# Shifted rows of a convolution loaded place and channel first, shift last, and issued by SP: an encoder trunk on one core

## The chip, the cores and the metric

The kernel runs on one core of one Trainium2 chip. The metric is device time in microseconds (us) of one execution, by the median of several runs. One more execution was taken with the hardware profiler; all rows below are of that one.

The engines have the names of the profile: PE is TensorE's matrix multiplication and PEld its weight load, DVE is VectorE, ACT is ScalarE, POOL is GpSimd. SP, SyncE, computes nothing and issues DMAs. A name with q (SPq, POOLq) is that engine's queue of instructions. Each engine works through its own instructions in order; a DMA, once issued, runs on the core's 16 DMA engines.

## The reference

A trunk of two layers on x of 512 tokens by 1024 channels, float32. Each layer is a half-step SwiGLU FFN, a token mixer, a second half-step FFN; every part has an RMSNorm before it and a residual add. Layer 0 mixes by a Conformer convolution, layer 1 by a bidirectional HGRN2 recurrence. The change lies in the convolution alone:

```python
def conformer_conv(h, w_pw1, b_pw1, w_dw, b_dw, ln_g, ln_b, w_pw2, b_pw2):
    a, gate = jnp.split(h @ w_pw1 + b_pw1, 2, axis=-1)
    u = a * jax.nn.sigmoid(gate)
    u = lax.conv_general_dilated(          # depthwise: 31 taps along the tokens
        u, w_dw[:, None, :], window_strides=(1,), padding=[(15, 15)],
        dimension_numbers=("NWC", "WIO", "NWC"), feature_group_count=1024) + b_dw
    u = layer_norm(u, ln_g, ln_b)
    return jax.nn.silu(u) @ w_pw2 + b_pw2
```

## The kernel before, in words

Channels lie on the 128 partitions, in 8 blocks of 128 (KD); the 512 tokens lie along the free dimension. Every weight matrix is split into a high and a low part (`split`, L137: a cast on ACT at L138, a subtraction on DVE at L139), and each product is three matmuls (`mm3`, L195, with lines L196 to L198). Weight chunks of up to 1 MB come through three buffers, issued by SP at L133 (`wdma`), about two chunks ahead of use. The high and low parts have three buffers each, so that a cast waits for matmuls of three parts ago.

The parts run one after the other: `ffn(0)`, `conv`, `ffn(1)`, `ffn(2)`, `hgrn`, `ffn(3)`.

In `conv` (L679) a loop over the 8 blocks j makes two projections of 24 matmuls each (`proj`, L415), `pa` and the gate `pg`. Then `evac` (L706) makes the gated block `u` on DVE and ACT, with even and odd tokens apart (L711 to L714); that of j = 0 is held until the statistics of the RMSNorm are there, after the third projection. `u` is 128 channels by 2 phases by 272 places.

The depthwise convolution is done by PE: for that, one partition has to hold one pair of place group and channel group at one of four shifts. `evac` gets this by a way over DRAM. It stores `u` to a DRAM tile `ud` of 32 rows (L721; the profile writes `ud<-u`), a row being one of 2 phases and one of 16 channel groups (CG), with 8 channels of 272 places (row = 2176 values). It then loads `u8` from it (L724; the profile writes `u<-ud`, leaving out the digit): each of the 32 rows four times, from four starting places one value apart, 2173 values each, which makes 128 partitions. `u8` has three buffers, `ud` two. POOL issues both for j = 0 to 6, and SP for j = 7. POOL also builds `w8` (L726), the taps' weights spread to a block form.

`taps_of` (L733) then runs 64 matmuls on PE in the profile (L738, 128x256 each) and puts their result, plus bias, into `y` (L752 or L754); `y` is stored into the `v` tiles (L776). Sums of `y` and its square are kept on POOL (`s1`, `s2`, L768 and L769) and brought over the partitions by small matmuls (`sums`, L780, line L789).

The order is set by `hook` (L795): after the fourth k of the first projection of a turn j, the oldest `u8` that waits in `ready` is taken, if there are two, so the taps of block j run in turn j + 2. The last three run behind the loop, with the sums of `s1` and `s2` ahead of the last (L805 to L808). The framework that builds the program may move an instruction some places against this order on its engine. After the last sums come the layer norm (L817 to L834), and `k_outer` with the second pointwise weights.

On the host, `_layout` (L1225) arranges the tap weights `tw` and the selection `ch` to fit the order of partitions of `u8`.

Of the kernel before, what the change touches and what calls it, by code (L numbers as in the profile page):

```python
# [18 lines left out]
P = 128  # L19
D = 1024  # L20
S = 512
KD = D // P
# [25 lines left out]
SH, CG = 8, 16  # L48
NG, NW = P // CG, 4
NM = 272  # L50
# [15 lines left out]
def tile_encoder(ctx: ExitStack, tc: tile.TileContext, xT, vecs, masks, w13, w2, pw1, kout, kout2, win, win_i, taps, out):  # L66
    nc = tc.nc
# [40 lines left out]
    for w_ in win_order:  # L108
        n = int(w_[1:])
# [153 lines left out]
    def col(c):  # L263
        return vec[:, c:c + 1]
# [122 lines left out]
    def rs():  # L387
        return norm["rs"]
# [290 lines left out]
    def conv(next_prep):  # L679
# [3 lines left out]
        with tc.tile_pool(name="cv", bufs=1) as cv, ExitStack() as scratch:  # L683
# [15 lines left out]
            def ap(t, off, dims, part=True):  # L699
                a = t[:]  # L700
                return bass.AP(a.tensor, a.offset + off, ([list(a.ap[0])] if part else []) + dims)

            def pairs(t):
                return t.rearrange("p (b h) -> p b h", h=2)

            def evac(j, pa, pg):  # L706
                ta = tp.tile([P, S], F32, name="t0", tag="t0")
                tg = tp.tile([P, S], F32, name="t1", tag="t1")
                sg = tp.tile([P, S], F32, name="t2", tag="t2")
                u = us[j % 3]  # L710
                nc.vector.tensor_tensor(tg, pg, rs(), op=ALU.mult)  # L711
                nc.scalar.activation(sg, tg, AF.Sigmoid, bias=col(C_BPW1 + 8 + j))
                nc.vector.tensor_tensor(ta, pa, rs(), op=ALU.mult)
                nc.vector.scalar_tensor_tensor(ap(u, 7, [[1, T2], [NM + 1, 2]]), pairs(ta), col(C_BPW1 + j), pairs(sg),  # L714
                                               op0=ALU.add, op1=ALU.mult)


                row = NG * NM
                e = nc.sync if j == KD - 1 else nc.gpsimd
                ud = dr.tile([2 * CG, row], F32, name="ud", tag="ud")  # L720
                e.dma_start(ap(ud, 0, [[NM, P], [CG * row, 2], [1, NM]], False), u)  # L721
                u8 = cp.tile([P, row], F32, name="u8", tag="u8", bufs=3)
                n = row - SH // 2 + 1
                e.dma_start(u8[:, :n], ap(ud, 0, [[1, SH // 2], [row, 2 * CG], [1, n]], False))  # L724
                w8 = cp.tile([P, NG * NW, 2 * CG], F32, name="w8", tag="w8", bufs=2)
                nc.gpsimd.tensor_tensor(w8.rearrange("p n (c h) -> p n c h", h=2),  # L726
                                        ap(cw, T_CH, [[0, NG * NW], [2, CG], [1, 2]]),
                                        ap(cw, T_W + j * NG * NW * 2, [[2, NG * NW], [0, CG], [1, 2]]), op=ALU.mult)
                ready.append((j, u8, w8))
# [70 lines left out]
            for j in range(KD):  # L800
                pa = proj(lead, xh, xl, hook)
                pg = proj(lead, xh, xl, hook)
                lead.evac(lambda j=j, pa=pa, pg=pg: evac(j, pa, pg))
# [421 lines left out]
def _layout(x, norm_g, ffn_w13, ffn_w2, conv_w_pw1, conv_b_pw1, conv_w_dw, conv_b_dw, conv_ln_g, conv_ln_b,  # L1225
            conv_w_pw2, conv_b_pw2, hgrn_w_in, hgrn_lb, hgrn_gn_g, hgrn_w_out, final_g):


    def cols(a):
        a = np.asarray(a).reshape(-1, KD, P)  # L1230
        return a.transpose(2, 0, 1).reshape(P, -1)

    lb = np.asarray(hgrn_lb).transpose(1, 0, 2)


    n = np.arange(D)
    back = n // P * P + n % 32 // 2 * NG + n % P // 32 * 2 + n % 2
    p, k, g, w, h = np.ix_(np.arange(P), np.arange(KD), np.arange(NG), np.arange(NW), np.arange(2))
    wpad = np.pad(np.asarray(conv_w_dw)[0], ((1, 2), (0, 0)))
    tw = wpad[SH * w + p // 32 * 2 + 1 - p % 32 // CG - h + 1, k * P + p % CG * NG + g].reshape(P, -1)  # L1240
    p1, c1 = np.meshgrid(np.arange(P), np.arange(P), indexing="ij")
    same = p1 % 2 == c1 % 2
    ch = p1[:, :2 * CG] % CG == c1[:, :2 * CG] // 2
    p, k, h = np.ix_(np.arange(P), np.arange(KD), np.arange(2))
    tb = np.asarray(conv_b_dw)[0][k * P + p % 32 // 2 * NG + p // 32 * 2 + h].reshape(P, -1)
    taps = np.concatenate([tw, same, ch, tb, same[:, :2]], axis=1, dtype=tw.dtype)
    vecs = np.concatenate([cols(norm_g), cols(final_g), cols(conv_b_pw1), cols(np.asarray(conv_ln_g)[..., back]),
                           cols(np.asarray(conv_ln_b)[..., back]), cols(conv_b_pw2), cols(lb), cols(hgrn_gn_g)], axis=1)
    s, t = np.meshgrid(np.arange(P), np.arange(P), indexing="ij")
    masks = np.zeros((P, 7, P), np.float32)  # L1250
    for l in range(7):
        masks[:, l] = (s ^ t) >> l == 1
    w13 = np.asarray(ffn_w13).reshape(4, NP, 2, P, 2, NFF, P).transpose(0, 5, 3, 4, 2, 1, 6).reshape(4, NFF, P, 2 * D)
    w2 = np.asarray(ffn_w2).reshape(4, 2, HALF, P, KD, P).transpose(0, 1, 4, 3, 2, 5).reshape(4, 2, KD, P, HALF * P)
    pw1 = np.asarray(conv_w_pw1)[0].reshape(KD, P, 2, KD, P).transpose(3, 1, 2, 0, 4).reshape(KD, P, 2 * D)
    kw = np.stack([np.asarray(conv_w_pw2)[0][back], np.asarray(hgrn_w_out)[0]]).reshape(2, 4, 2, P, KD, P)
    kout = kw[:, :, :, :, :NOUT].transpose(0, 1, 3, 2, 4, 5).reshape(2, 4, P, 2 * NOUT * P)
    kout2 = kw.reshape(2, KD, P, KD, P)[:, :, :, NOUT:].transpose(0, 2, 3, 1, 4).reshape(2, P, 2 * D)
    wi = np.asarray(hgrn_w_in)[0].reshape(KD, P, 5, NH, P)
    win = wi[:, :, [0, 2, 3, 4]].reshape(KD, P, 2, 2, NH, P).transpose(4, 2, 1, 3, 0, 5).reshape(NH, 2, P, 2 * D)  # L1260
    win_i = np.asarray(hgrn_w_in)[0][:, D:2 * D].reshape(2, 4, P, 2, S).transpose(3, 0, 2, 1, 4)
    win_i = win_i.reshape(4, P, 2 * D)
    xT = np.asarray(x)[0].T.reshape(KD, P, S)
    arrays = dict(xT=xT, vecs=vecs, masks=masks.reshape(P, 7 * P), w13=w13, w2=w2, pw1=pw1, kout=kout, kout2=kout2,
                  win=win, win_i=win_i, taps=taps)
    return {k: np.ascontiguousarray(v) for k, v in arrays.items()}
# [19 lines left out]
```

## Time and profile before

| | |
|---|---|
| runs | 2082.84, 2089.87, 2090.8 us; median 2089.87 |
| the profiled execution | 2090.77 us, of which the span is 2089.0 |
| PE busy | 1965.5 us (94%) |
| DVE busy | 1457.9 us (70%) |
| ACT busy | 964.9 us (46%) |
| POOL busy | 156.0 us (7%) |
| mean granted TensorE clock | 0.972 of full speed |
| loads of `u8` on POOL | 7 of 1086.5 KB, median 23.4 us from issue to landing |

The span is the time from the first to the last instruction that the profiler shows. Busy shares are means over the whole span: stages with different limits lie in them. DMA-issuing instructions are not counted as busy. "Landing" is the end of a transfer, counted from its issue. The granted clock is the share of full TensorE clock that the throttle allowed in a stretch.

### The profile page before, as it was taken

How to read it: one execution, taken by the hardware profiler on the slowest of the kernel's cores; microseconds unless marked ns; L12 is line 12 of the kernel's file. 1: busy time of each engine (PE TensorE's matmuls, PEld its weight loads, DVE VectorE, ACT ScalarE, POOL GpSimd, SP SyncE). 2: the span in 40 equal slices, each digit the busy share in tenths (PEclk: the TensorE clock that was granted, in tenths of full speed). 3: DMA queues.
4: the chain of work that ended last, by engine and by line, in shares of the span. 5: the costliest groups of instructions: out<-in, count | busy, mean ns of one | idle time of the engine just before them, and what ended most of it. 6: DMA issues, size and time to landing. Idle time of an engine off the chain costs nothing.

```text
span 2089.0 us, 31116 instructions
## 1 busy us (share of the span) xinstructions
PE 1965.5 (94%) x12767; PEld 1758.1 (84%) x12767; DVE 1457.9 (70%) x2207; ACT 964.9 (46%) x1593; POOL 156.0 (7%) x129
## 2 busy tenths in 40 slices
PE   8999999667589999999999999999999999999997
PEld 7998998544367998998998999888888878989996
DVE  7965975323158965978994796568857878947964
ACT  5643653211045643654662464345545545634642
POOL 2000001122101000001000000111101110000002
PEclk9999999888789999999999999999999999999998
DMA  5223233333312223223223232321111121233221
GB/s 192 81 84 108 101 100 113 121 93 97 106 66 81 102 84 109 101 100 113 96 95 104 101 108 91 117 79 61 61 62 71 43 89 61 99 105 110 102 97 55
DMA packets 40274, 196.47 MB, mean 94 GB/s; under 512 B 6740, under 2 KB 13268, under 8 KB 24132
## 3 DMA queue, kind: packets, MB, share of 16 engines
q1 hardware_dynamic: 33092, 181.57, 25.3%
q0 software_dynamic: 4480, 10.56, 1.9%
q10 hardware_dynamic: 2560, 2.36, 0.4%
q8 instruction: 100, 1.64, 0.3%
q14 instruction: 42, 0.34, 0.0%
HBM read 188.04 MB, written 4.33 MB: 92 GB/s over the span
## 4 chain that ended last, share of the span: by engine, by line
PE 65%; DVE 5%; issue 1%; ACT 1%; DVEq 0%; ACTq 0%
PE mm L511 28%; PE mm L196 9%; PE mm L198 9%; PE mm L197 9%; PE aux L983 3%; PE mm L444 2%; DVE wlo L139 1%; PE mm L886 1%; PE mm L888 1%; PE mm L887 1%; PE aux L1055 1%; DVE x7l L460 1%; PE aux L292 0%; ACT whi L138 0%; DVE bl L460 0%
## 5 line engine op out<-in xcount | busy, mean ns | idle before, releaser
L511 PE MATMUL mm<-x7h,whi 128*128 128x256 f32 x1944 | 546.7, 282 | 7.1 <-ACT mm L524 3.5
L511 PE MATMUL mm<-x7h,wlo 128*128 128x256 f32 x1944 | 545.2, 281 | 2.4 <-DVE wlo L139 2.3
L511 PE MATMUL mm<-x7l,whi 128*128 128x256 f32 x1944 | 545.6, 281 | 1.4 <-DVE x7l L158 1.4
L138 ACT CAST whi<-wraw 128x1024 fp32r<-128x1024 f32 (+2 forms) x297 | 274.3, 924 | 362.2 <-PE mm L197 311.7
L139 DVE TENSOR_TENSOR wlo<-wraw,whi 128x1024 fp32r<-128x1024 f32 (+2 forms) x297 | 324.3, 1092 | 144.9 <-ACT whi L138 140.3
L511 PEld LDWEIGHTS mm<-x7h,whi 128*128 128x128 f32 x1944 | 366.2, 189 | 10.1 <-ACT mm L524 4.4
L511 PEld LDWEIGHTS mm<-x7h,wlo 128*128 128x128 f32 x1944 | 366.2, 189 | 3.6 <-DVE wlo L139 3.6
L511 PEld LDWEIGHTS mm<-x7l,whi 128*128 128x128 f32 x1944 | 366.4, 188 | 2.2 <-DVE x7l L158 2.0
L196 PE MATMUL mm<-gh,whi 128*128 128x512 f32 (+1 forms) x715 | 276.0, 386 | 0.0
L198 PE MATMUL mm<-gh,wlo 128*128 128x512 f32 (+1 forms) x715 | 275.9, 386 | 0.0
L197 PE MATMUL mm<-gl,whi 128*128 128x512 f32 (+1 forms) x715 | 275.9, 386 | 0.0
L138 ACT CAST whi<-s 128x1024 fp32r<-128x1024 f32 x162 | 169.9, 1049 | 168.3 <-PE mm L511 117.3
L139 DVE TENSOR_TENSOR wlo<-s,whi 128x1024 fp32r<-128x1024 f32 x162 | 197.9, 1222 | 40.7 <-ACT whi L138 40.1
L370 POOL TENSOR_TENSOR ss<-ss,sq 128x512 f32<-128x512 f32 x48 | 67.0, 1396 | 1465.7 <-ACT sq L369 1464.9
L198 PEld LDWEIGHTS mm<-gh,wlo 128*128 128x128 f32 x715 | 134.3, 188 | 27.1
L196 PE MATMUL mm<-xh,whi 128*128 128x512 f32 x384 | 156.8, 408 | 0.0
L196 PEld LDWEIGHTS mm<-gh,whi 128*128 128x128 f32 x715 | 134.3, 188 | 26.6
L197 PEld LDWEIGHTS mm<-gl,whi 128*128 128x128 f32 x715 | 134.3, 188 | 26.3
L198 PE MATMUL mm<-xh,wlo 128*128 128x512 f32 x384 | 152.3, 397 | 0.0
L197 PE MATMUL mm<-xl,whi 128*128 128x512 f32 x384 | 150.8, 393 | 0.0
L158 DVE TENSOR_TENSOR s<-wraw 128x512 f32<-128x512 f32 x162 | 110.5, 686 | 8.5 <-DMA wraw<-in_w 6.6
L638 DVE TENSOR_TENSOR t<-mm,rs 128x512 f32<-128x512 f32 x63 | 43.5, 691 | 104.4 <-PE mm L198 104.4
(245 smaller groups left out, 3223.0 us busy)
## 6 DMA issues: line engine op xcount, KB each, us to landing
wraw<-in_w SPq DMA_DIRECT2D x87, 1024.0 KB, 4.8
wraw<-in_w SPq DMA_DIRECT2D x64, 704.0 KB, 4.1
wraw<-in_win SPq DMA_DIRECT2D x16, 1024.0 KB, 4.8
wraw<-in_pw SPq DMA_DIRECT2D x8, 1024.0 KB, 4.8
u<-ud POOLq DMA_DIRECT2D x7, 1086.5 KB, 23.4
wraw<-in_kout SPq DMA_DIRECT2D x8, 768.0 KB, 7.1
wraw<-in_win_i SPq DMA_DIRECT2D x4, 1024.0 KB, 4.6
x<-in_xT SPq DMA_DIRECT2D x8, 256.0 KB, 6.0
```

What stands on the lines that cost most here:

```text
L138: nc.scalar.copy(hi[:, a:b], raw[:, off + a:off + b])
L139: nc.vector.tensor_tensor(lo[:, a:b], raw[:, off + a:off + b], hi[:, a:b].bitcast(F32), op=ALU.subtract)
L158: nc.vector.tensor_tensor(o, a, b, op=op)
L196: nc.tensor.matmul(o, lhsT=wh, rhs=ah, start=first, stop=False)
L197: nc.tensor.matmul(o, lhsT=wh, rhs=al, start=False, stop=False)
L198: nc.tensor.matmul(o, lhsT=wl, rhs=ah, start=False, stop=last)
L370: nc.gpsimd.tensor_tensor(norm["ss"], norm["ss"], sq, op=ALU.add)
L444: nc.tensor.matmul(o[:, x[0]], lhsT=wt[:, sl], rhs=x[at], start=k == 0 and wt is w[0] and at == 1 and x is ops[0], stop=k == KD - 1 and wt ...
L460: nc.vector.scalar_tensor_tensor(l, xs[k][:, c], col(gc + k), h.bitcast(F32), op0=ALU.mult, op1=ALU.subtract)
L511: nc.tensor.matmul(o, lhsT=a[:, sl], rhs=b[kp][:, x], start=start and kp == 0 and a is w[0] and b is x7h, stop=kp == NP - 1 and a is w[1], ...
L638: nc.vector.tensor_tensor(pn, p, norm["rs05"], op=ALU.mult)
L983: nc.tensor.matmul(sp[:, c * P:(c + 1) * P], lhsT=kp[:, c * P:(c + 1) * P], rhs=view(Q, hl, c), start=True, stop=True)
```

## The change

The load of `u8` reads the same values, in another order of partitions: before, the shift was the slowest index (partition = 32 x shift + row), after, the row is (partition = 4 x row + shift). The store and the load of every block are issued by SP. The host tables follow the new order of partitions; their sizes stay.

```diff
                 row = NG * NM
-                e = nc.sync if j == KD - 1 else nc.gpsimd
                 ud = dr.tile([2 * CG, row], F32, name="ud", tag="ud")
-                e.dma_start(ap(ud, 0, [[NM, P], [CG * row, 2], [1, NM]], False), u)
+                nc.sync.dma_start(ap(ud, 0, [[NM, P], [CG * row, 2], [1, NM]], False), u)
                 u8 = cp.tile([P, row], F32, name="u8", tag="u8", bufs=3)
                 n = row - SH // 2 + 1
-                e.dma_start(u8[:, :n], ap(ud, 0, [[1, SH // 2], [row, 2 * CG], [1, n]], False))
+                nc.sync.dma_start(u8[:, :n], ap(ud, 0, [[row, 2 * CG], [1, SH // 2], [1, n]], False))
...
-    tw = wpad[SH * w + p // 32 * 2 + 1 - p % 32 // CG - h + 1, k * P + p % CG * NG + g].reshape(P, -1)
+    tw = wpad[SH * w + p % 4 * 2 + 1 - p // 64 - h + 1, k * P + p // 4 % CG * NG + g].reshape(P, -1)
...
-    ch = p1[:, :2 * CG] % CG == c1[:, :2 * CG] // 2
+    ch = p1[:, :2 * CG] // 4 % CG == c1[:, :2 * CG] // 2
```

## Rows read from the trace of the kernel before

**Rows 1.** The page: granted TensorE clock in 40 equal slices, in tenths.

```profile
PEclk9999999888789999999999999999999999999998
```

**Rows 2.** Waits, 355 to 680 us: who waited for whom, us in total, times, longest.

```profile
PE mm L738 <- DMA u<-ud: 73.3, 7, 20.7
...
POOL u L724 <- DMA ud<-u: 63.7, 7, 20.6
```

**Rows 3.** Groups by line, 365 to 582 us: the taps matmuls.

```profile
L738 PE MATMUL mm<-u,w 128*32 128x256 f32 x512 | 44.8, 516 | 73.3 <-DMA u<-ud 73.3
```

**Rows 4.** PE in order of time: start us, us; in brackets idle time before.

```profile
394.23 0.39 PE L197 MATMUL mm<-xl,whi 128*128 128x512 f32 x1
394.45 0.39 PE L198 MATMUL mm<-xh,wlo 128*128 128x512 f32 x1
413.46 4.91 PE L738 MATMUL mm<-u,w 128*32 128x256 f32 x64 [18.62 <-DMA u<-ud]
...
449.83 0.39 PE L198 MATMUL mm<-xh,wlo 128*128 128x512 f32 x1
...
535.06 0.39 PE L198 MATMUL mm<-xh,wlo 128*128 128x512 f32 x1
536.84 3.66 PE L738 MATMUL mm<-u,w 128*32 128x256 f32 x64 [1.39 <-DMA u<-ud]
...
569.77 1.87 PE L789 MATMUL aux<-cw,s 128*128 128x2 f32 x8 [2.46 <-POOL s L768]
...
574.36 6.36 PE L738 MATMUL mm<-u,w 128*32 128x256 f32 x62
```

**Rows 5.** POOL in order of time, its stores and loads.

```profile
388.61 0.77 POOL L721 DMA_DIRECT2D ud<-u  x1 [12.27 <-DVE u L714]
...
392.91 0.76 POOL L721 DMA_DIRECT2D ud<-u  x1 [0.66 <-DVE u L714]
...
453.71 0.79 POOL L721 DMA_DIRECT2D ud<-u  x1 [6.35 <-DVE u L714]
```

**Rows 6.** SP's queue in order of time.

```profile
397.04 0.33 SPq L133 DMA_DIRECT2D wraw<-in_pw  x1
...
448.47 0.33 SPq L133 DMA_DIRECT2D wraw<-in_pw  x1
...
538.24 0.38 SPq L721 DMA_DIRECT2D ud<-u  x1
540.71 0.67 SPq L724 DMA_DIRECT2D u<-ud  x1
```

**Rows 7.** Landing of the DMAs of L721, L724, and L133 (365 to 585).

```profile
DMA to landing us min/median/max: 2.3/8.2/21.1
...
DMA to landing us min/median/max: 21.8/23.4/24.9
...
DMA to landing us min/median/max: 4.6/12.4/13.6
```

**Rows 8.** Windows: length, engines' busy us, granted clock, DMA share, GB/s.

```profile
272.00:274.00 2.00, 2.00 (x19) 2.00 (x18) 1.97 (x3) 0.57 (x1) 0.00 (x0) 1.00 0.91 385
...
365.00:585.00 220.00, 142.35 (x952) 102.43 (x950) 56.62 (x77) 34.22 (x43) 44.83 (x39) 0.81 0.37 101
...
404.00:410.00 6.00, 0.00 (x0) 0.00 (x0) 0.00 (x0) 0.00 (x0) 0.00 (x0) 0.50 0.27 102
546.00:560.00 14.00, 0.00 (x0) 0.00 (x0) 0.00 (x0) 0.00 (x0) 0.00 (x0) 0.50 0.51 121
```

**Rows 9.** DMA issues by line: size of each, median us to landing.

```profile
wraw<-in_pw SPq DMA_DIRECT2D x8, 1024.0 KB, 4.8
...
u<-ud POOLq DMA_DIRECT2D x7, 1086.5 KB, 23.4
...
ud<-u SPq DMA_DIRECT2D x1, 272.0 KB, 2.3
```

**Rows 10.** ACT in order of time: the cast of a weight part.

```profile
500.31 1.05 ACT L138 CAST whi<-wraw 128x1024 fp32r<-128x1024 f32 x1 [4.37 <-PE mm L197]
```

## The prediction

> **What bounds the kernel now.** I read the page first. The slices show the granted TensorE clock at 9 tenths nearly everywhere and a dip to 7 and 8 in slices 8 to 12 [rows 1]: something starves TensorE between about 365 and 600 us, and that is the convolution (L679), where every changed line runs. So the argument is made in that stage alone.
>
> Next the waits from 355 to 680 us. On PE one dominates: the taps matmuls of L738 wait for the DMA that fills `u8`, seven times, 73.3 us, the longest 20.7 [rows 2]. The groups by line from 365 to 582 us give the matmuls' own time: 512 in 44.8 us, that is 5.6 us for each of the eight `taps_of` [rows 3]. The order of PE's work shows what that should be: with 1.39 us of idle time before them, 64 took 3.66 us; after 18.62 us of idle time 4.91 [rows 4]. While PE sits idle the clock falls: in 404 to 410 and in 546 to 560, with no matmul at all, the granted clock is 0.50, the lower of the two levels (1.2 against 2.4 GHz) [rows 8]. So the late loads cost twice, as waits and as slow taps.
>
> Then, why the loads are late. On POOL the first store goes at 388.61, the second at 392.91 with the first load between them, a later one at 453.71 [rows 5]. A load took 21.8 to 24.9 us to land, a store 2.3 to 21.1, median 8.2, and the load always waits for its store [rows 7]. The windows say why the load is slow: from 404 to 410, with this one load in flight, the sixteen DMA engines were busy 0.27 of the time and moved 102 GB/s, which is four engines' worth; from 546 to 560, with two such loads in flight, 0.51 and 121 GB/s; yet from 272 to 274, in a weight load, 0.91 and 385 GB/s [rows 8]. The load's outermost dimension in L724 is the shift, of size 4. A weight chunk of nearly the same size (1024 against 1086.5 KB) lands in 4.8 us, the load in 23.4 [rows 9].
>
> The Trainium skill, DMA: Bandwidth & Descriptors, section "Why a DMA increments its semaphore by 16 and not by 1", says a DMA runs on the largest number of engines, up to 16, that divides the slowest dimension of both sides. By that the old order gets 4 and the new (32 outermost) gets 16; the trace agrees on the 4, and no run yet shows the 16.
>
> **The change part by part.**
>
> *The order of the load.* Same bytes, same 128 rows of 8.7 KB, but place and channel (32) outermost and shift innermost. Lower bound for the load: a weight chunk's 4.8 us [rows 9], 5.1 for 1086.5 KB. Upper bound: nothing gained, 23.4. Between: if what holds two loads at 121 GB/s is not the number of engines but the small region that they read, 1.11 MB take 9.2 us. Quartering 23.4 for four times the engines gives 5.9. I take 5.9, near the weight chunk, because per engine 102 GB/s over four is what 385 GB/s over sixteen is (25 and 24).
>
> *Issue on SP.* Seven stores and seven loads leave POOL for SP; the eighth pair is on SP already. On SP that store (272 KB) landed in 2.3 us [rows 9], with the load following 2.47 us after it (538.24, 540.71) [rows 6]; I take 2.5. POOL loses 7 x 2 issues and 63.7 us of waiting between them [rows 2], and nothing on POOL sets the end, so I cost that at nothing; what hides it is that POOL's sums for `s1`, `s2` are needed only at L807.
>
> On SP each load waits for its store, and behind the waiting load stand the weight loads of L133. Pair j can be issued about 3.7 us after the second projection of j (last matmul 449.83 to 450.06, store 453.71) [rows 4, 5], the weight chunk of that turn goes out earlier, at 448.47 [rows 6]; a chunk behind the pair would be held for at most 2.5 us plus two issues. That chunk's second half was first cast in the turn that ends at 500.31 [rows 10]: 52 us later, and still about 30 at the faster pace below. I cost it at nothing.
>
> *When the data is wanted.* From the end of the second projection of j to taps j, PE has 60 projection matmuls (12 up to taps j - 1, the other 36 of that turn, 12 of the next; the starts 394.23 and 394.45 are one step apart, 0.227 us over a run of them, so 13.6 us [rows 4]) and one taps block of 3.66: 17.3 us. The chain to be hidden is 3.7 (to the store) + 2.5 + 0.1 + load. With 5.9 it is 12.2, so there is no wait in the middle, with 5.1 us to spare; a load of up to 11.0 us would do. Now it is about 3.7 + 8.2 + 0.3 + 23.4 = 35.6, which is why each turn waits. VectorE is no bound in place of it: 56.6 us busy in the 220 from 365 to 585 [rows 8], against some 130 that the stage would still take.
>
> *First taps.* Store at 388.4, load at 390.9, landed at 396.8; PE stops at 394.84 as before [rows 4]: 2.0 us left of 18.62.
>
> *Last taps.* The second projection of j = 7 ends at 535.29. Chain to the last taps: 2.95 (store at 538.24) + 2.5 + 5.9 = 11.3 us. Before them PE has two taps blocks (7.3), then waits 2.46 us for POOL's sum as now and runs 16 small matmuls of L789 (1.87 for the first eight at the low clock, perhaps half that at the high one) [rows 4]: about 0.6 us of wait is left, and the L789 give back some 1.9.
>
> **The sum.** Waits 73.3, less 2.0 at the first taps: 71.3. Taps at full clock: 44.8 - 8 x 3.66 = 15.5. Around the last taps: 1.9 - 0.6 = +1.3. Together 88 us. The profiled execution took 2090.77 (span 2089.0, 1.8 around it), 0.9 above the median of the three runs shown (2089.87). 2090.8 - 88 = 2002.8. I forecast **2003 us**. What comes after (from 581 us) is moved, not changed.
>
> Own range: with the load at 5.1, 1.5 less; if the clock also stays high over the short gaps ahead of the pointwise projection, 2 x 1 us on L292 and some 3 on its first matmuls less: 1997. With 9.2, 3.3 us at each end and some slow matmuls: 2011. If on SP the first pair stands behind the weight chunk that went out at 397.04 [rows 6], 6 to 8 us more: 1997 to 2016.
>
> **The rivals.**
>
> *Same queue, same ring (12 in 100).* Pairs and weight chunks now share SP's queue. On POOL one store took 21.1 us to land, the longest; the second, at 392.91, was issued right behind the first load and is the one that fits [rows 5, 7]: it stood behind that load. If each pair stands behind a whole weight chunk (4.8), the chain is 17.0 against 17.3: no wait in the middle, but 4.8 at each end: 2003 + 9.6 = 2012.6.
> The Trainium skill's same page, "Queues, rings and completion order", says each engine takes descriptors of one queue in ring order but alternates between queues; by it this price is real, and the 21.1 us agree.
>
> *Spread, but slow (8 in 100).* Weight chunks landed at a median of 12.4 us in this stage [rows 7], though spread over all engines. If the loads take 13, the chain is 19.3, 2 us over the cover, which two successive waits share: 1 us each, four times. At the ends 7.1 twice, and 5 for slow taps there: 2003 + 23 = 2026. Against: what delayed those chunks was the four busy engines, which the change clears.
>
> *The order does nothing (5 in 100).* The one load on SP in the trace, old order, was no faster: issued at 540.71, and the DMA was still half busy up to 560 [rows 6, 8]. If 23.4 stays, only the stores gain: the chain is 29.7, two successive waits share 12.4, so 6.2 each instead of 8.1 (73.3 less 18.62, 1.39 and 20.7, over four): 4 x 2 saved; the first taps save nothing, the last some 10: 2072.
>
> *Slower (2 in 100).* SP, held by a pair, delays a weight chunk until PE wants it. It decides only where a chunk is held more than 30 - 5 = 25 us; to eat 88 us over eight turns and 10 more it must be 25 + 12 = 37 in each, that is SP standing behind a load whose `u8` buffer (three of them) is freed by taps not yet run, in every turn: 2101. Against: that buffer was read two turns before.
>
> **How the numbers follow.** The forecast itself has 73 in 100. 10 us (0.5%) is about what a measurement of this kernel can tell from no change; the three runs spread over 8. All cases but the last are faster by more: 0.96; within 0.5%: 0.02; slower: 0.02. The range 1995 to 2024 holds the forecast, the shared ring and half of the slow spread.
>
> **What would show it.** Landing of the L724 loads near 6 us and DMA share near 0.9 while one runs; PE's wait for `u` down from 73.3 to under 8 us, in one or two waits at the ends; L738 at about 30 us for 512; clock at 9 tenths through slices 8 to 10; taps 14.6 us apart instead of 24 to 26; the last taps near 493 instead of 580.7. I am wrong if loads land above 11 us, if SP's wait for `ud` shows weight casts late behind it, or if PE's taps are placed elsewhere in its order and meet loads that are still on the way.

## The result, and the profile after

The changed kernel takes 2005.66 us (median; 2003.07 to 2006.75), the kernel before 2089.27 beside it: a ratio of 0.9604, 95% interval 0.9581 to 0.9626. The forecast was 2003 us, with 1995 to 2024 as its range.

The page of the changed kernel: the span, PE's busy time, the granted clock in 40 slices.

```profile
span 2003.5 us, 31105 instructions
...
PE 1949.3 (97%) x12767; PEld 1749.6 (87%) x12767; DVE 1454.9 (73%) x2207; ACT 964.6 (48%) x1593; POOL 144.7 (7%) x115
...
PEclk9999999999899999999999999999999999999998
```

Against [rows 1] the dip of the clock in five slices has shrunk to one slice at 8 tenths. PE's busy time fell too, by 16 us, though it has the same 12767 matmuls: 14.9 of it is in the stage of the convolution below, where matmuls had run at the low clock.

Where the time came from is read by splitting both executions behind the last taps (windows; the first row is of the kernel after, the second fence of the kernel before; columns as in [rows 8]).

```profile
365.00:496.40 131.40, 125.14 (x932) 93.36 (x930) 51.40 (x71) 32.02 (x41) 33.60 (x23) 0.97 0.47 166
...
496.40:2003.50 1507.10, 1471.14 (x9473) 1331.05 (x9473) 1130.17 (x1744) 749.88 (x1253) 88.17 (x66) 0.99 0.25 89
```

```profile
365.00:581.40 216.40, 139.99 (x936) 100.24 (x934) 55.26 (x71) 32.30 (x41) 44.83 (x39) 0.81 0.37 101
...
581.40:2089.00 1507.60, 1471.45 (x9473) 1331.33 (x9473) 1130.13 (x1745) 750.18 (x1253) 88.89 (x66) 0.99 0.26 89
```

The stage of the convolution shrank from 216.4 to 131.4 us, by 85.0; what follows is as long as it was (1507.6 and 1507.1). In the stage PE's idle time fell from 76.4 to 6.3 us and its busy time from 140.0 to 125.1: 70.2 and 14.9, together the 85.0. Its mean granted clock went from 0.81 to 0.97.

The waits of the kernel after, from 355 to 585 us, and its taps in the groups by line, 365 to 500 us (L737 is L738 of before):

```profile
PE mm L737 <- DMA u<-ud: 3.0, 2, 1.7
...
PE aux L788 <- POOL s L767: 2.5, 1, 2.5
```

```profile
L737 PE MATMUL mm<-u,w 128*32 128x256 f32 x512 | 31.8, 397 | 3.0 <-DMA u<-ud 3.0
```

Of the 73.3 us of [rows 2] 3.0 are left, and the taps' 44.8 us of [rows 3] are 31.8. PE in order of time shows where the rest of both sits:

```profile
395.69 3.66 PE L737 MATMUL mm<-u,w 128*32 128x256 f32 x64 [1.67 <-DMA u<-ud]
...
423.27 3.66 PE L737 MATMUL mm<-u,w 128*32 128x256 f32 x64
437.96 3.66 PE L737 MATMUL mm<-u,w 128*32 128x256 f32 x64
...
485.08 1.05 PE L788 MATMUL aux<-cw,s 128*128 128x2 f32 x8 [2.46 <-POOL s L767]
487.51 1.06 PE L737 MATMUL mm<-u,w 128*32 128x256 f32 x2 [1.38 <-DMA u<-ud]
...
490.30 5.35 PE L737 MATMUL mm<-u,w 128*32 128x256 f32 x62
```

In the middle, taps blocks stand 14.7 us apart with no wait and take 3.66 us each. At the end PE waits twice, and the last block runs slow: the granted clock is 0.50, the lower level, from 487 to 493.

SP's queue of the kernel after, one turn, and the landing of the stores (L720) and of the loads (L723):

```profile
409.14 0.36 SPq L720 DMA_DIRECT2D ud<-u  x1
411.62 0.53 SPq L723 DMA_DIRECT2D u<-ud  x1
417.97 0.34 SPq L133 DMA_DIRECT2D wraw<-in_pw  x1
```

```profile
DMA to landing us min/median/max: 2.2/2.3/4.5
...
DMA to landing us min/median/max: 5.0/5.6/7.6
```

Against [rows 7] the median load went from 23.4 to 5.6 us. In a window in which the load of that turn was on the way, with two `v` stores of 128 KB beside it:

```profile
413.00:417.00 4.00, 4.00 (x19) 3.33 (x18) 1.74 (x3) 1.69 (x2) 3.86 (x3) 1.00 0.92 308
```

All sixteen engines are nearly always busy (0.92, against the 0.27 of [rows 8]) and move 308 GB/s in place of 102. The 102 are not the load's alone, though: of the 0.61 MB moved from 404 to 410 in the kernel before, 0.25 went through the queue of hardware DMAs, where the weight chunk of 397.04 was, and 0.37 through POOL's, where the load was.

### The profile page after: what moved, and what is told of

Its sections match the earlier page's. It is cut to its first block, busy times and chain, and to the rows that moved or that the text cites. A ratio compares the mean times of both kernels' runs of the same rounds, so it can differ in the third digit from the quotient of the medians.

```text
span 2003.5 us, 31105 instructions
## 1 busy us (share of the span) xinstructions
PE 1949.3 (97%) x12767; PEld 1749.6 (87%) x12767; DVE 1454.9 (73%) x2207; ACT 964.6 (48%) x1593; POOL 144.7 (7%) x115
## 4 chain that ended last, share of the span: by engine, by line
PE 87%; DVE 7%; ACT 2%; issue 2%; DMA 1%; POOL 0%; SPq 0%; DVEq 0%; ACTq 0%; POOLq 0%
PE mm L511 39%; PE mm L196 12%; PE mm L198 12%; PE mm L197 12%; PE mm L444 3%; PE aux L982 2%; DVE wlo L139 1%; PE mm L737 1%; PE mm L885 1%; PE mm L886 1%; PE mm L887 1%; PE aux L1054 1%; ACT whi L138 1%; DVE x7l L460 1%; PE aux L292 1%
```

## The experiments

The change has two parts. Does one alone do it, and which?

**The order alone.** The changed kernel, with POOL as issuer again.

```diff
+                e = nc.sync if j == KD - 1 else nc.gpsimd
-                nc.sync.dma_start(ap(ud, 0, [[NM, P], [CG * row, 2], [1, NM]], False), u)
+                e.dma_start(ap(ud, 0, [[NM, P], [CG * row, 2], [1, NM]], False), u)
-                nc.sync.dma_start(u8[:, :n], ap(ud, 0, [[row, 2 * CG], [1, SH // 2], [1, n]], False))
+                e.dma_start(u8[:, :n], ap(ud, 0, [[row, 2 * CG], [1, SH // 2], [1, n]], False))
```

> The new order of the load, issued by POOL as before (SP only for the last block). Theory (the slowest dimension of the load decides how many DMA engines work on it; 32 in place of 4 is the whole change): the loads land in 6 to 8 us on POOL too, the chain from the end of a second projection is 3.7 + 3 + 7 = 14 of 17.3 us, no wait in the middle: 2004 to 2012 us. Rival (the move to SP is what counts, POOL's queue makes stores and loads late): stores at 8 us and loads above 11, waits stay, 2040 us or more.

Measured: 2007.06 us, ratio 0.9613 (0.9596 to 0.963). The interval and that of the change overlap. Landing of its stores, then of its loads (seven on POOL and the last on SP):

```profile
DMA to landing us min/median/max: 2.6/2.7/4.9
...
DMA to landing us min/median/max: 5.3/5.8/7.6
```

So the order is all of the gain that can be measured. The stores were late on POOL (8.2 in [rows 7]) not because of POOL: with the new order they land there in 2.7 us.

**SP alone.** The kernel before, with SP as issuer.

```diff
-                e = nc.sync if j == KD - 1 else nc.gpsimd
+                e = nc.sync
```

> The old order of the load, all stores and loads issued by SP. Theory (number of engines): loads still near 20 us and more, DMA share near 0.25 while one runs, only the stores gain: 2060 to 2085 us. Rival (SP is what counts): loads under 11 us, 2004 to 2015 us. Third possibility: weight chunks share the queue with the four busy engines and come late, above 2090 us.

Measured: 2094.84 us, ratio 1.003 (1.0017 to 1.0044): slightly slower than before, the time of the third possibility. SP's queue, one turn; then the DMA issues of the stores (KB, median us to landing); then PE's wait for `u`:

```profile
472.28 0.36 SPq L721 DMA_DIRECT2D ud<-u  x1
482.87 0.53 SPq L724 DMA_DIRECT2D u<-ud  x1
```

```profile
ud<-u SPq DMA_DIRECT2D x8, 272.0 KB, 10.4
```

```profile
PE mm L738 <- DMA u<-ud: 77.0, 7, 19.3
```

The load follows its store by 10.6 us; on POOL it was 7.9 to 10.6 in the turns in the middle. The load of the turn before, issued at 457.98, is still under way: the taps that wait for it start at 480.59, and two microseconds later the store, which stands behind it in the same queue, has landed too. The weight chunks, with the pairs now in their queue, landed in a median of 14.9 us from 365 to 585, in place of 12.4 [rows 7]. But no engine waited for one of them in the stage, so the reason given for the third possibility is not what cost the time: PE's wait for `u` grew, from 73.3 to 77.0 us.

Then: is it the order in which neighbours are read, or the number of engines? Two kernels cross the two.

**Old order of partitions, one DMA for each shift** (against the kernel before).

```diff
-                e = nc.sync if j == KD - 1 else nc.gpsimd
+                e = nc.sync
...
-                e.dma_start(u8[:, :n], ap(ud, 0, [[1, SH // 2], [row, 2 * CG], [1, n]], False))
+                for s in range(SH // 2):
+                    e.dma_start(u8[32 * s:32 * s + 32, :n], ap(ud, s, [[row, 2 * CG], [1, n]], False))
```

> The old order of partitions (shift slowest), on SP, but as four DMAs, one for each shift, of 32 rows each, so that the shift is in no DMA a dimension. Theory (number of engines by the slowest dimension of one DMA): each runs on 16 engines, all four have landed some 7 us after the first issue (5.6 and three more issues of 0.5): 2005 to 2010 us. Rival (it is the order in which neighbours are read, place first and shift last, that makes it fast): near the run with the old order on SP, 2060 or more.

Measured: 2008.65 us, ratio 0.9621 (0.9601 to 0.964). Each of the four lands in a median of 5.7 us; PE waits 7.1 us for `u`, at the first and the last taps only:

```profile
PE mm L739 <- DMA u<-ud: 7.1, 2, 3.6
```

**New order of partitions, DMAs of four rows** (against the changed kernel).

```diff
-                nc.sync.dma_start(u8[:, :n], ap(ud, 0, [[row, 2 * CG], [1, SH // 2], [1, n]], False))
+                for i in range(8):
+                    nc.sync.dma_start(u8[16 * i:16 * i + 16, :n],
+                                      ap(ud, 4 * i * row, [[row, 4], [1, SH // 2], [1, n]], False))
```

> The new order of partitions (shift fastest), on SP, but as eight DMAs of 4 rows by 4 shifts each, so that the slowest dimension of each is 4 again. Theory (number of engines): all eight on 4 engines, landed 14 to 24 us after the first issue, waits for u back, 2030 to 2080 us. Rival (the order itself): as fast as the changed kernel but for seven more issues of 0.5 us, 2006 to 2012 us.

Measured: 2045.8 us, ratio 0.9799 (0.9784 to 0.9814). A window in which little but its loads was on the way:

```profile
408.00:414.00 6.00, 6.00 (x62) 3.95 (x54) 0.76 (x2) 1.23 (x4) 1.94 (x1) 0.91 0.25 103
```

A quarter of the engines with the new order too, and with waits for `u` back (32.5 us on three): the share goes with the size of the outermost dimension of one DMA (0.25 at 4, 0.92 at 32), not with the order. This kernel still beats the one before: where PE waited for a load in the middle, it used it 17.1 us after the first issue (425.64 to 442.72), where the old order took 22.6 on SP.

The order has a part of its own in that. In a window of the run with the old order on SP, with the load alone on the way, the same quarter of the engines moved about half as much:

```profile
436.00:438.00 2.00, 2.00 (x15) 1.38 (x8) 0.88 (x2) 0.53 (x1) 1.39 (x1) 1.00 0.23 56
```

In the traces, one row of 8.7 KB held its engine for a median of 583 to 642 ns in the three kernels with the old order, on four engines or sixteen, and 328 ns in every kernel with the new one. From its first packet to its last, the load took 17 to 22 us with the old order on four engines (SP), 11 to 13 with the new order on four, 5.7 to 7.6 with the old on sixteen and 3.4 to 4.3 with the new on sixteen. So the number of engines is the larger part, and the order adds a second; with sixteen engines either load is hidden in the middle, and the second part shows only at the ends (7.1 us of wait against 3.0, three more issues for each load among it). Why a row takes longer in the old order no run here shows.

**DMAs of eight rows**, for a value in between.

```diff
+                for i in range(4):
+                    nc.sync.dma_start(u8[32 * i:32 * i + 32, :n],
+                                      ap(ud, 8 * i * row, [[row, 8], [1, SH // 2], [1, n]], False))
```

> The new order on SP as four DMAs of 8 rows by 4 shifts, so that the slowest dimension is 8. Theory (number of engines, and a cover of some 17 us that hides a load of up to 11 us): eight engines at the 25 GB/s of each in the kernel before, 5.5 us, with the fixed part and three more issues landed some 9 us after the first issue; DMA share near 0.5; no wait in the middle, 3 us more at each end than in the changed kernel: 2008 to 2016 us. Rival (nothing is hidden once a load takes more than the weight chunk's 5 us): 3 us more in each of eight turns, 2028 us or more.

Measured: 2012.17 us, ratio 0.9629 (0.9612 to 0.9646). Its first and last taps:

```profile
399.07 5.71 PE L739 MATMUL mm<-u,w 128*32 128x256 f32 x64 [5.04 <-DMA u<-ud]
...
497.28 3.21 PE L739 MATMUL mm<-u,w 128*32 128x256 f32 x28 [3.66 <-DMA u<-ud]
```

The six blocks between have no wait: 8.7 us of wait in all, 5.7 more than the changed kernel, at the two ends. From 420 to 422 the DMA share was 0.59 with 204 GB/s. A load of some 9 us (first issue 416.78, last packet done at 425.9) is still hidden in the middle, as a cover of 17 us minus 6 of chain says.

**Less cover.** The changed kernel with the taps asked for a turn earlier.

```diff
-TAPS_AT = 4
+TAPS_AT = 12
...
-                if turn[0] % 16 == TAPS_AT and len(ready) > 1 and turn[0] < 16 * (KD - 1):
+                if turn[0] % 16 == TAPS_AT and len(ready) > 0 and turn[0] < 16 * (KD - 1):
```

> The changed kernel with the taps of a block asked for one turn earlier (the built order puts them 36 to 48 projection matmuls behind the block's second projection, 8.2 to 10.9 us, some with a taps block of 3.7 more, where it was 60 and one block, 17.3). Theory (chain of 11 to 12 us from the end of the second projection to the landed load, waits are what the cover lacks): some 3 us of wait where the cover is 36, 1 or none at 48, 5 more at the first taps, 4 more at the last: 2012 to 2024 us. Rival (the loads are no longer near the edge, waits at the ends only): 2005 to 2008 us.

Measured: 2018.68 us, ratio 0.9657 (0.9638 to 0.9676). PE waits 12.2 us for `u`, five times; four of its eight taps:

```profile
396.40 5.09 PE L737 MATMUL mm<-u,w 128*32 128x256 f32 x64 [7.17 <-DMA u<-ud]
...
445.57 3.66 PE L737 MATMUL mm<-u,w 128*32 128x256 f32 x64 [1.62 <-DMA u<-ud]
457.55 3.66 PE L737 MATMUL mm<-u,w 128*32 128x256 f32 x64
475.90 3.66 PE L737 MATMUL mm<-u,w 128*32 128x256 f32 x64 [1.10 <-DMA u<-ud]
```

Waits are back in the middle. They are small: 1.0 to 1.6 us where the built order (that of the built program, which the framework may have moved) has 48 projection matmuls (10.9 us) as the cover, and none where it has 36, since there the taps block before and its own wait stand in between too (at 457.55: 8.2 + 3.66 + 1.62 = 13.5 us). I had expected 3 us there, and had left the block out. Both say that the chain is about 12 us. The changed kernel's own rows say it too: the second projection of that turn ended 12 matmuls ahead of the taps of 408.57, at 405.85; the load went out at 411.62 and took 5.6, in all 11.4.

**What is left at the end.** Two versions try to remove it. First, the sums of `s1` and `s2` behind the last taps:

```diff
-            sums((s1, 0), (s2, 4))
...
+                    sums((s1, 0), (s2, 4))
                     sums((y, 0), (sq, 4))
```

> The changed kernel with the sums of s1 and s2 over the partitions behind the last taps in place of ahead of them. Theory (what is left at the end is POOL's sum, 2.46 us, in front of taps whose load lands soon after): the last taps start when their load lands, near 487.4 in place of being cut in two by the sums, and end some 3 to 4 us earlier: 2001 to 2003.5 us. Rival (the load and the clock set the end, not the sums): no change beyond 1 us.

Measured: 2001.36 us, ratio 0.9581 (0.9564 to 0.9598), beside 0.9604 of the change. The built order still put the first eight small matmuls ahead of the last taps, with their 2.46 us of wait; the taps ran in one piece from 488.06 and ended at 493.2, in place of 495.65. The interval overlaps that of the change. Second, the same with more cover for the last load:

```diff
-                u8 = cp.tile([P, row], F32, name="u8", tag="u8", bufs=3)
+                u8 = cp.tile([P, row], F32, name="u8", tag="u8", bufs=4)
...
-                if turn[0] % 16 == TAPS_AT and len(ready) > 1 and turn[0] < 16 * (KD - 1):
+                if turn[0] % 16 == TAPS_AT and len(ready) > 1 and turn[0] < 16 * (KD - 2):
```

> As the run with the sums last, and u8 with four buffers and no taps in turn 6, so that three taps blocks stand between the last projection and the last taps and cover the last load. Theory: the last second projection ends 3.7 us earlier, its load lands 3.7 us earlier too, the three blocks fill the time, PE waits under 2 us: 7 to 9 us less than the changed kernel, 1997 to 2000 us. Rival (the y tiles, the v stores or POOL's sums become the wait at the end): no better than the run with the sums last.

Measured: 1998.73 us, ratio 0.9564 (0.9547 to 0.9581). The end of its taps:

```profile
470.74 10.57 PE L737 MATMUL mm<-u,w 128*32 128x256 f32 x192
482.55 3.66 PE L737 MATMUL mm<-u,w 128*32 128x256 f32 x64 [1.24 <-DMA u<-ud]
486.71 1.05 PE L789 MATMUL aux<-cw,s 128*128 128x2 f32 x8 [0.50 <-POOL s L767]
```

Three blocks cover the last load, the last block is at full clock and ends at 486.2. To compare it with the changed kernel on one chip, both ran once more:

> The changed kernel as it is, beside the next run on the same chip: 2003 to 2008 us.

> The run with the sums last and four u8 buffers once more, beside the changed kernel. Theory (the cover of the last load and POOL's sum are what is left of the waits): 6 to 8 us below the changed kernel, with intervals that do not meet. Rival: the earlier difference came from the chips, under 2 us apart.

Measured: 2005.23 us, ratio 0.9606 (0.9586 to 0.9625), and 1999.15 us, ratio 0.9574 (0.9552 to 0.9595). The medians are 6.1 us apart, as expected, and the runs of the two don't overlap (2003.7 to 2007.05, 1995.93 to 2002.35), but the intervals meet by 0.0009, against what I had expected; both are ratios to the same nine runs of the kernel before, whose spread is in each. So the version is likely the fastest of all here, by 0.3% of the changed kernel's time, and that is at the edge of what this measurement tells.

## Why the prediction was right

*The bound* was right: the convolution's stage holds the whole difference, 85.0 of the 85.5 us between the spans.

*The load's time* was the term that everything hung on: 5.9 us forecast, 5.6 measured. Its reason, four engines and then sixteen, is shown by the crossing: 0.23 to 0.25 of the DMA with either order of partitions where the outermost dimension is 4, and 2005.7 to 2008.7 us with either order where it is 32. The rule of the Trainium skill that was cited (DMA: Bandwidth & Descriptors, "Why a DMA increments its semaphore by 16 and not by 1") names that dimension; the run with 8 fits it too (0.59 and 204 GB/s).

The rate behind the 5.9 was misread, and its fit is in part luck. I took the 102 GB/s from 404 to 410 as one load's, 25 GB/s for each of four engines, as for a weight chunk; a weight chunk was in that window as well, and the load alone moved 52 to 70 GB/s on such a quarter in the run with SP alone. That the order also makes each row faster (583 to 328 ns) was in no term; the half rate could have been seen in [rows 8], where two loads at a share of 0.51 moved 121 GB/s together. With more engines and no faster rows, the load would have been that of the run with one DMA for each shift: 4.1 us more of wait at the two ends, inside the range.

*The cover* was right: 17.3 us against a chain of 12.2 forecast, some 11.4 measured, no wait in the middle; a load of 9 us changed nothing there, and less cover brought waits back.

*The sum.* Waits: 71.3 forecast, 70.3 measured (73.3 - 3.0). Taps at full clock: 15.5 forecast, 13.0 measured (44.8 - 31.8). This term was mis-sized: I put all eight blocks at 3.66 us, and the last ran 5.35 and 1.06 behind the two waits at the end. Around the last taps 1.3 forecast; measured, 0.8 us from the shorter sums (3.7 to 2.9 us in the groups by line). 84.1 in all, where 88 were forecast and the spans differ by 85.5; of the rest, 1.1 us is PE's busy time in the stage outside the taps and these sums (14.9 less 13.0 and 0.8).

*The issue on SP* was given a part that it does not have. I put the stores' fall from 8.2 to 2.5 us down to SP, and took the one store on SP in the trace, with no load ahead of it, as the price. The stores were late because the load of the turn before was still on the way: with the old order they took 10.4 us on SP, with the new one 2.7 on POOL. The sum came out near because the order removes that cause as well; that part is luck.

For the same reason the rival "the order does nothing" had the right mechanism and the wrong price: 2072 forecast, 2094.84 measured, since its stores took 10.4 us and not 2.5, and no wait was saved (77.0 us against 73.3). *The same ring* was seen only once in the changed kernel, in the second store (4.5 us, the longest), behind the first load; in the turns in the middle weight chunks and pairs follow each other on SP at some 6 us, as in the rows above (409.14, 411.62, 417.97).

## What to carry to other kernels

A DMA share of a quarter with one transfer in flight says that four of sixteen engines work: look at the outermost dimension of that transfer, and reorder it or split it into DMAs that have a large one. Read the GB/s beside the share, and with one transfer alone in the window: the same quarter of the engines moved some 60 or 103 GB/s, by the order in which the rows were read. Such a transfer also delayed the others here, whatever issued them, so what looks like a slow issuer (stores at 8 us) can be the slow load's shadow. Before crediting a load's gain, write down the chain up to its use and the work that covers it: only the part that sticks out is time, and here also the clock that PE loses while it waits.

## What was not expected

While the slow load ran, transfers in all queues were late: with the old order the `v` stores on ACT took a median of 14.7 us, with the new one 4.0 (DMA issues, kernel before and after), and the weight chunks of the stage 12.4 and 4.7:

```profile
v<-y ACTq DMA_DIRECT2D x14, 128.0 KB, 14.7
```

```profile
v<-y ACTq DMA_DIRECT2D x14, 128.0 KB, 4.0
```

And POOL as issuer cost nothing that can be seen: 5.7 us for a load against 5.6 on SP, 2.7 for a store against 2.3.
